# Weight splits and load-dependent work pinned in traced order, stores of split pairs two weights later, first loads reordered

## The chip, the cores and the metric

One core of a Trainium2 chip runs the kernel. Its engines are TensorE (PE in the profile; PEld are its weight loads), VectorE (DVE), ScalarE (ACT), GpSimd (POOL) and SyncE (SP, which here only issues DMAs). The metric is the device time of one execution in microseconds (us). Before the change it is 2699.4 us, the median of three runs from 2695.46 to 2699.83.

## The reference

One layer of a hybrid decoder, in float32, for a prompt of 2048 rows and a sample batch of 8 x 4 rows. The width D is 1024, the MLP's is 4096.

```python
xn = rms_norm(x, norm_mix_pre)
qk_raw, v_m, o_m, gates, q_a, k_a, v_a = split_projection(xn @ w_in)
y_m = mlstm_output(mlstm(short_conv(qk_raw), v_m, gates), o_m, mlstm_norm)
y_a = rms_norm(sliding_window_attention(q_a, k_a, v_a, attn_sinks), attn_norm)
x = x + rms_norm(concatenate([y_m, y_a]) @ w_out, norm_mix_post)
u = rms_norm(x, norm_ffn_pre)
f = square(relu(u @ w_up)) @ w_down
x = x + rms_norm(f, norm_ffn_post)
x = x + sigmoid(x @ w_pgate) * (p @ w_pproj)
```

The new recurrent states and attention caches are outputs too. (The calls in the third and fourth line are shortened.)

## The kernel before

**Products in three passes.** A float32 product is made of values split into a rounded part and a rest: `hi = round(v)`, `lo = v - hi`. TensorE then adds hi x hi, hi x lo and lo x hi (`mm3`). So every weight tile is split once (`wsplit`, L247): ACT casts it to hi (L248), DVE or POOL subtracts (L249). `weng` (L242) gives the subtraction to DVE and POOL in turn, unless the caller names one.

**The ring of weights.** `Ring` hands out the split pairs in the order of a plan that covers the whole program. There are PAIRS = 7 slots of pairs and RAWS = 5 of raw loads. `take(n)` (L323) makes as many weights ready as LOOK or LOOKR say beyond n; both are 0, so a weight's load and split are traced where it is used. A weight that is used again is stored as a pair in DRAM (`keep`, L266, the DMA `wk<-w` at L268 on POOL's queue) and loaded from there later (`w<-wk`, L274, SP). Tiles are named by their number in the ring: w305 is the pair, wr310 a raw load, wb3130 and wb3131 are the two wide raw tiles of an up step, 302 to 312 the weights of step 5 of the first group, and re050, hh0500, hl0510, dn0511 belong to that step.

**Stages.** The 16 blocks of 128 prompt rows are projected in six chunks (w_in, attention and mLSTM, up to about 700 us). Then come three groups of blocks, each with the output projection (`mix`), the MLP and the gated embedding (`gate`). The first group makes and stores its split weights, the two others load them. The MLP has 16 steps; each multiplies two column blocks of w_up and adds into f through two row blocks of w_down. From step FAST on (2, 4 and 2 in the three groups) the two chunks of a group share seven products instead of eight (`up_both`, L1670): sums of the weights' quarters are built by POOL and DVE (`Ring.product`, L284) and sums of the activations by `sums()` (L1620). The fourth product's weight (key 3) makes two pairs from one quarter: first a by-product, `self.last`, then a subtraction on POOL (L303), then the pair itself.

**What sets the order.** `Flow.issue` pins TensorE's instructions in traced order (`keep_in_program_order`). All other instructions are put in order by a scheduler below the kernel, engine by engine, and each engine and queue then runs its own strictly in that order. Side work (`mix_post`, `gate_post`, `gate_embed`, `sums`, attention, mLSTM) are generators; each `yield` says how many us of TensorE's work are traced before it goes on.

**Also touched.** `fetch` and `project` load and norm the prompt rows (the scaling of a block is at L584, its factor x0t on POOL at L499, the sum of squares on ACT at L497, SP's load at L456). `weights` in the mLSTM adds a mask to Wt (L927) behind a load. The sample's state work loads `sso` (L1255, POOL's queue) and takes a tanh (L1256, ACT). `finish` (L1792) stores the outputs, `gate_embed` (L1830) loads and transposes p.

## Time and profile before

| | |
|---|---|
| median of three runs | 2699.4 us |
| the profiled execution's own time | 2696.58 us |
| its span | 2694.8 us |
| mean granted TensorE clock | 0.979 |
| instructions | 39194 |
| DMA | 626.98 MB, mean 233 GB/s |

The profile shows one execution. A row of a timeline has the start, the length, the engine, the line and operation, out<-in without numbers, and in brackets the idle time before it with what ended it. A row of waits has an engine's line, what released it, the total, the number of times and the longest. The granted clock is a share of full speed; the kernel's 0.979 is a mean over stretches at full and at half speed. TensorE's busy time counts instructions that run at half clock as busy.

### The profile page before, as it was taken

The numbers are of one execution on the slowest core, as the hardware profiler recorded it, in microseconds if no ns is written. First come the engines' busy times: TensorE is split into PE (matmuls) and PEld (weight loads), VectorE is DVE, ScalarE is ACT, GpSimd is POOL, SyncE is SP. The second block draws the span as 40 slices with busy tenths as digits, with TensorE's granted clock in tenths as the row PEclk, the third lists the DMA queues.
The fourth block names the chain that finished last, engine by engine and source line by source line (L and its number), as shares of the span: only waits on it lengthen the run. The fifth ranks groups of instructions, "written<-read, shape, count | busy, mean of one in ns | idle before, by whom it ended". The sixth has DMA issues, their size and how long they took to land.

```text
span 2694.8 us, 39194 instructions
## 1 busy us (share of the span) xinstructions
PE 2550.8 (95%) x14284; PEld 2221.0 (82%) x14284; DVE 1475.1 (55%) x3112; ACT 982.1 (36%) x2163; POOL 635.4 (24%) x928
## 2 busy tenths in 40 slices
PE   4899999999899999999898998999999998999997
PEld 4788878788678888888787887889998878999985
DVE  3665756655667666666643446444446345444452
ACT  3554554544545444433422423222223133222241
POOL 3510111112434666665623130000001010000010
PEclk9899999999899999999999998999999999999999
DMA  7756566576786666665798731555556896777786
GB/s 235 272 204 209 196 195 212 187 263 238 260 316 210 254 248 252 247 248 220 273 354 274 253 93 56 172 188 193 188 188 223 299 328 220 256 256 257 259 293 218
DMA packets 219409, 626.98 MB, mean 233 GB/s; under 512 B 33141, under 2 KB 65097, under 8 KB 219200
## 3 DMA queue, kind: packets, MB, share of 16 engines
q1 hardware_dynamic: 173392, 465.77, 51.4%
q0 software_dynamic: 45776, 158.68, 15.2%
q8 instruction: 113, 1.85, 0.3%
q14 instruction: 80, 0.66, 0.1%
q10 hardware_dynamic: 48, 0.03, 0.0%
HBM read 470.22 MB, written 155.25 MB: 232 GB/s over the span
## 4 chain that ended last, share of the span: by engine, by line
PE 68%; DVE 9%; DMA 7%; issue 7%; POOL 5%; ACT 3%; SPq 0%; POOLq 0%; DVEq 0%; ACTq 0%
PE dn L145 18%; PE up L145 18%; PE mo L145 5%; PE pg L145 4%; PE v L145 3%; PE o L145 2%; POOL w L249 2%; PE qk L145 2%; PE gv L145 2%; PE qa L145 1%; PE aT L149 1%; PE aO L145 1%; DMA wk<-w 1%; DVE hl L228 1%; PE aS L145 1%
## 5 line engine op out<-in xcount | busy, mean ns | idle before, releaser
L145 PE MATMUL dn<-w,hh 128*128 128x512 f32 x1792 | 572.3, 401 | 22.6 <-DVE f L1718 16.9
L145 PEld LDWEIGHTS dn<-w,hh 128*128 128x128 f32 x1792 | 335.3, 191 | 105.6 <-DVE f L1718 23.1
L1718 DVE TENSOR_TENSOR f<-f,dn 128x512 f32<-128x512 f32 x420 | 285.8, 686 | 221.4 <-PE dn L145 220.9
L145 PE MATMUL dn<-w,hl 128*128 128x512 f32 x896 | 356.8, 398 | 4.3 <-DVE hl L228 4.1
L1682 DVE TENSOR_TENSOR re<-up,re 128x384 f32<-128x384 f32 (+1 forms) x280 | 144.0, 514 | 289.3 <-PE up L145 289.2
L145 PEld LDWEIGHTS dn<-w,hl 128*128 128x128 f32 x896 | 170.4, 190 | 45.4 <-DVE hl L228 5.9
L268 POOL DMA_DIRECT2D wk<-w x242 | 133.9, 555 | 108.4 <-DVE w L249 85.3
L1683 ACT COPY re<-up 128x384 f32<-128x384 f32 (+1 forms) x40 | 17.9, 448 | 379.6 <-PE up L145 379.6
L228 DVE TENSOR_TENSOR hl<-re,hh 128x384 fp32r<-128x384 f32 (+1 forms) x192 | 120.3, 627 | 62.3 <-ACT hh L227 61.6
L1608 ACT ACTIVATE re<-re 128x384 f32<-128x384 f32 (+1 forms) x160 | 78.8, 493 | 170.6 <-DVE re L1682 168.3
L248 ACT CAST w<-wb 128x512 fp32r<-128x512 f32 x98 | 60.6, 621 | 200.9 <-PE dn L145 128.4
L248 ACT CAST w<-wr 128x512 fp32r<-128x512 f32 (+1 forms) x152 | 93.6, 620 | 103.2 <-issue 22.3
L249 POOL TENSOR_TENSOR w<-wr,w 128x512 fp32r<-128x512 f32 (+1 forms) x76 | 103.1, 1357 | 95.0 <-ACT w L248 87.2
L1432 POOL TENSOR_TENSOR f<-f,gffn 128x512 f32<-128x512 f32 x16 | 21.0, 1321 | 430.2 <-ACT j L1430 429.8
L249 POOL TENSOR_TENSOR w<-wb,w 128x512 fp32r<-128x512 f32 x70 | 90.1, 1298 | 106.8 <-ACT w L248 106.4
L249 DVE TENSOR_TENSOR w<-wr,w 128x512 fp32r<-128x512 f32 (+1 forms) x76 | 80.3, 1058 | 43.6 <-ACT w L248 41.1
L1026 DVE CUSTOM_DVE_ANT_0 s<-aS,cst,sink 128x256 f32<-128x256 f32 (+1 forms) x128 | 56.9, 472 | 75.4 <-PE aS L145 75.2
L1609 ACT ACTIVATE re<-re 128x384 f32<-128x384 f32 (+1 forms) x192 | 94.9, 495 | 6.0
L227 ACT CAST hh<-re 128x384 fp32r<-128x384 f32 (+1 forms) x192 | 92.5, 482 | 6.8
L1032 ACT ACTIVATE s<-s,swt 128x257 f32<-128x257 f32 (+1 forms) x128 | 63.3, 496 | 72.3 <-DVE swt L1029 71.4
L145 PE MATMUL up<-ut11h,w 128*128 128x384 f32 x320 | 88.8, 340 | 0.0
L1615 POOL CAST hh<-hh 128x16 fp32r<-128x16 f32 x32 | 7.1, 222 | 338.2 <-ACT hh L227 338.1
(1525 smaller groups left out, 6538.6 us busy)
## 6 DMA issues: line engine op xcount, KB each, us to landing
w<-wk SPq DMA_DIRECT2D x678, 512.0 KB, 4.8
wk<-w POOLq DMA_DIRECT2D x238, 512.0 KB, 5.8
wr<-in_w_down_dram SPq DMA_DIRECT2D x64, 256.0 KB, 6.8
wb<-in_w_up_dram SPq DMA_DIRECT2D x28, 512.0 KB, 5.8
w<-wk SPq DMA_DIRECT2D x20, 528.0 KB, 4.1
x<-in_x_prompt_dram SPq DMA_DIRECT2D x16, 512.0 KB, 4.2
y<-yd SPq DMA_DIRECT2D x32, 256.0 KB, 5.8
xr<-in_x_prompt_dram SPq DMA_DIRECT2D x16, 512.0 KB, 9.2
```

The lines of the kernel that those rows point to most:

```text
L145: ins = self.pe.matmul(out, lhsT, rhs, start=start, stop=stop)
L227: act.copy(hi, src)
L228: dve.tensor_tensor(lo, src, hi.bitcast(F32), ALU.subtract)
L248: act.copy(hi, src)
L249: (eng or weng()).tensor_tensor(lo, src, hi.bitcast(F32), ALU.subtract)
L268: put(self.kept[key], t.bitcast(U32))
L1026: dve.tensor_tensor_reduce(s_[:, s, lo : 2 * P], pS[:, s, lo:], bias[:, j, lo:], 1.0 if s == 0 else 0.0625, sink[:, h : h + 1], ALU.add, A ...
L1032: act.activation(e_, e_, AF.Exp, bias=nm[:, s : s + 1], accum_out=sm[:, s : s + 1])
L1608: act.activation(t, src, AF.Relu)
L1609: act.square(t, t)
L1682: add = lambda out, a, b: dve.tensor_tensor(out, a, b, ALU.add)
L1718: dve.tensor_tensor(out(i), out(i), ps[i], ALU.add)
```

## The change

- `wsplit` pins both halves of a split, and `Ring.take` makes AHEAD = 2 weights beyond those asked for, everywhere. So a split stands where it is traced, two weights before its use.
- `Ring.keep` no longer stores at once: `store` issues a pair's DMA when STORE = 2 more tiles were taken, pinned too.
- The first chunk's x1 and x2 are loaded ahead of the first weights, and normed later.
- Pinned as well: the mask add of Wt, the copies of the attention caches to the output, the tanh of sso.
- In `sums()`, the seven adds of the second half (q = 1) go from DVE to POOL in the second and third group.
- `finish` stores the last chunk's outputs from SP's queue; `gate_embed` loads all tiles of p first, yields EMBW = 3.0 us, and then transposes.

Where instructions stand now, at three places. The first is DVE's queue at the start of the program (x0t is the norm factor of block 0, x00t its first transpose, w2 to w6 are weights of the gates and values and of the attention's queries). Before:

```order
L498 TENSOR_SCALAR x0t_181<-x0t_181 128x1
L249 TENSOR_TENSOR w2_195<-wr2_196,w2_195 128x528
L249 TENSOR_TENSOR w4_211<-wr4_212,w4_211 128x528
L498 TENSOR_SCALAR x1t_223<-x1t_223 128x1
L498 TENSOR_SCALAR x2t_231<-x2t_231 128x1
L249 TENSOR_TENSOR w6_386<-wr6_387,w6_386 128x512
L584 SCALAR_TENSOR_TENSOR x0_90<-x0_90,x0t_181,gpre_159 128x1024
L228 TENSOR_TENSOR x0l0_239<-x00t_241,x0h0_237 128x4x128
L228 TENSOR_TENSOR x0l1_240<-x01t_248,x0h1_238 128x4x128
L584 SCALAR_TENSOR_TENSOR x1_221<-x1_221,x1t_223,gpre_159 128x1024
```

Now:

```order
L507 TENSOR_SCALAR x0t_181<-x0t_181 128x1
L507 TENSOR_SCALAR x1t_243<-x1t_243 128x1
L507 TENSOR_SCALAR x2t_249<-x2t_249 128x1
L593 SCALAR_TENSOR_TENSOR x0_90<-x0_90,x0t_181,gpre_159 128x1024
L251 TENSOR_TENSOR w2_198<-wr2_199,w2_198 128x528
L593 SCALAR_TENSOR_TENSOR x1_187<-x1_187,x1t_243,gpre_159 128x1024
L593 SCALAR_TENSOR_TENSOR x2_189<-x2_189,x2t_249,gpre_159 128x1024
L251 TENSOR_TENSOR w4_213<-wr4_215,w4_213 128x528
L230 TENSOR_TENSOR x0l0_257<-x00t_259,x0h0_255 128x4x128
L230 TENSOR_TENSOR x0l1_258<-x01t_266,x0h1_256 128x4x128
L251 TENSOR_TENSOR w6_231<-wr6_233,w6_231 128x512
```

The scaling of x0, which TensorE's first transpose reads, stood behind the splits of w2, w4 and w6; it stands ahead of all of them now, behind the factors of x1 and x2.

The second is ACT's queue in step 5 of the first group's MLP, at the end of the down pass of step 4 and the first products of step 5 (up051 is the first product, w305 and its by-product w306 come from key 3). Before:

```order
L248 CAST w304_10115<-wb3020_10068 128x512
L1608 ACTIVATE re040_9768<-re040_9768 128x384
L1609 ACTIVATE re040_9768<-re040_9768 128x384
L227 CAST hh0410_9934<-re040_9768 128x384
L248 CAST w306_10137<-wb3021_10070 128x512
L248 CAST w305_10136<-wb3021_10070 128x512
L248 CAST w307_10181<-wb3020_10068 128x512
L248 CAST w308_10207<-wb3021_10070 128x512
L1683 COPY re050_10062<-up051_10066 128x384
L248 CAST w309_10232<-wr309_10233 128x512
```

Now:

```order
L250 CAST w304_10079<-wb3020_9966 128x512
L1696 COPY re050_10074<-up051_10078 128x384
L250 CAST w306_10102<-wb3021_9968 128x512
L250 CAST w305_10100<-wb3021_9968 128x512
L1620 ACTIVATE re051_10075<-re051_10075 128x384
L1621 ACTIVATE re051_10075<-re051_10075 128x384
L229 CAST hh0500_10124<-re051_10075 128x384
L250 CAST w307_10144<-wb3020_9966 128x512
L250 CAST w308_10163<-wb3021_9968 128x512
```

The casts of w305 to w308 stood ahead of re050, the evacuation of the first product; they stand behind it now.

The third is DVE's queue at the end of the same products and the start of the down pass (up053 is the last product; dn0500 is the first down product, its weights are w309 and w310). Before:

```order
L249 TENSOR_TENSOR w310_10239<-wr310_10240,w310_10239 128x512
L1682 TENSOR_TENSOR re050_10062<-up056_10114,re050_10062 128x384
L228 TENSOR_TENSOR hl0500_10111<-re051_10063,hh0500_10110 128x384
L1682 TENSOR_TENSOR re052_10064<-up057_10135,re050_10062 128x384
L249 TENSOR_TENSOR w312_10253<-wr312_10254,w312_10253 128x512
L1682 TENSOR_TENSOR re053_10065<-up054_10158,re052_10064 128x384
L249 TENSOR_TENSOR w313_10361<-wb3130_10362,w313_10361 128x512
```

and, three rows further on:

```order
L249 TENSOR_TENSOR w314_10384<-wb3131_10364,w314_10384 128x512
L1682 TENSOR_TENSOR re050_10062<-up053_10206,re050_10062 128x384
L228 TENSOR_TENSOR hl0511_10203<-re052_10064,hh0511_10202 128x384
L1718 TENSOR_TENSOR f0_7746<-f0_7746,dn0500_10260 128x512
L228 TENSOR_TENSOR hl0510_10229<-re050_10062,hh0510_10228 128x384
L1718 TENSOR_TENSOR f1_7747<-f1_7747,dn0501_10268 128x512
L1718 TENSOR_TENSOR f2_7748<-f2_7748,dn0502_10276 128x512
```

Now:

```order
L1695 TENSOR_TENSOR re050_10074<-up055_10189,re050_10074 128x384
L1695 TENSOR_TENSOR re050_10074<-up053_10217,re050_10074 128x384
L230 TENSOR_TENSOR hl0511_10214<-re052_10076,hh0511_10213 128x384
L251 TENSOR_TENSOR w310_10218<-wr310_10220,w310_10218 128x512
L230 TENSOR_TENSOR hl0510_10241<-re050_10074,hh0510_10240 128x384
L1731 TENSOR_TENSOR f0_7758<-f0_7758,dn0500_10272 128x512
L251 TENSOR_TENSOR w312_10251<-wr312_10253,w312_10251 128x512
L251 TENSOR_TENSOR w313_10258<-wb3130_10260,w313_10258 128x512
L251 TENSOR_TENSOR w314_10267<-wb3131_10262,w314_10267 128x512
L1731 TENSOR_TENSOR f1_7759<-f1_7759,dn0501_10280 128x512
L1731 TENSOR_TENSOR f2_7760<-f2_7760,dn0502_10288 128x512
```

w310's low half stood behind the second product's evacuation and stands behind the last one's now; those of w312, w313 and w314 stood among the products and stand between f0 and f1 now. On POOL, the first sum of the wide tiles of the step after next (wb3240, L298, traced two steps ahead) stood behind w311's low half and stands ahead of it now. On ACT, the tanh of sso stood between the evacuations f6 and f7 of the second group's output projection (L1521) and stands 82 rows further on, in the MLP.

```diff
--- before.py
+++ after.py
@@ -67,8 +67,9 @@
 MIXW = 6.0
 LODVE = 2
 STEPS = FF // (FS * P)
-LOOK = 0
-LOOKR = 0
+AHEAD = 2
+STORE = 2
+EMBW = 3.0
 RAWS, PAIRS = 5, 7
 
 
@@ -199,6 +200,7 @@
     pe = Flow(tc)
     swa, mls, tsp = pe.side(), pe.side(), pe.side()
     dma, put = nc.sync.dma_start, nc.gpsimd.dma_start
+    here = tc.keep_in_program_order
 
     xp = A["x_prompt"].rearrange("b t d -> (b t) d")
     xs = A["x_sample"].rearrange("b t d -> (b t) d")
@@ -245,8 +247,8 @@
         return dve if turns % LODVE == 0 else pool
 
     def wsplit(hi, lo, src, eng=None):
-        act.copy(hi, src)
-        (eng or weng()).tensor_tensor(lo, src, hi.bitcast(F32), ALU.subtract)
+        here(act.copy(hi, src))
+        here((eng or weng()).tensor_tensor(lo, src, hi.bitcast(F32), ALU.subtract))
 
     class Ring:
 
@@ -256,7 +258,7 @@
             self.raw = es.enter_context(tc.tile_pool(name=nm + "raw", bufs=raws))
             self.pair = es.enter_context(tc.tile_pool(name=nm + "pair", bufs=pairs))
             self.n = 0
-            self.plan, self.ready, self.kept, self.uses = None, [], {}, {}
+            self.plan, self.ready, self.kept, self.uses, self.later = None, [], {}, {}, []
 
         def tile(self, n):
             self.n += 1
@@ -265,11 +267,18 @@
 
         def keep(self, key, t):
             self.kept[key] = dram.tile(list(t.shape), U32, name=f"{self.nm}k{len(self.kept)}")
-            put(self.kept[key], t.bitcast(U32))
+            self.later.append((self.n, key, t))
+
+        def store(self):
+
+            while self.later and self.later[0][0] + STORE <= self.n:
+                _, key, t = self.later.pop(0)
+                here(put(self.kept[key], t.bitcast(U32)))
 
         def get(self, key, n, make):
 
             t = self.tile(n)
+            self.store()
             if key in self.kept:
                 dma(t.bitcast(U32), self.kept[key])
             else:
@@ -322,7 +331,7 @@
 
         def take(self, n=1):
 
-            while len(self.ready) < n + (LOOK if n > 2 else LOOKR):
+            while len(self.ready) < n + AHEAD:
                 key, make = next(self.plan, (None, None))
                 if make is None:
                     break
@@ -598,8 +607,9 @@
     def fetch(ci):
 
         for b in CHUNKS[ci]:
+            if b not in xq:
+                xq[b] = load_x(xp[b * P : (b + 1) * P, :], P, f"x{b}")
             if b > 0:
-                xq[b] = load_x(xp[b * P : (b + 1) * P, :], P, f"x{b}")
                 norm_x(xq[b], P, f"x{b}")
         if ci == len(CHUNKS) - 1:
             xq["s"] = load_x(xs, NS, "xs")
@@ -634,6 +644,8 @@
 
         if ci == 0:
             norm_x(xq[0], P, "x0")
+            for b in blocks[1:]:
+                xq[b] = load_x(xp[b * P : (b + 1) * P, :], P, f"x{b}")
         wg = by2(ring.take(4))
         Kh = pw.tile([P, 2, (CMAX + 1) * P], F32R, tag="Kh", name=f"Kh{ci}", bufs=2)
         Kl = pw.tile([P, 2, (CMAX + 1) * P], F32R, tag="Kl", name=f"Kl{ci}", bufs=2)
@@ -924,7 +936,7 @@
         def weights(i):
             Wt = sm.tile([P, MH, P], F32, tag="Wt", name=f"Wt{blocks[i]}")
             dma(Wt, bc(r["mbd"][:, i * P : (i + 1) * P], 0, P))
-            dve.tensor_tensor(Wt, Wt, bc(mask, 1, MH), ALU.add)
+            here(dve.tensor_tensor(Wt, Wt, bc(mask, 1, MH), ALU.add))
             for h in range(MH):
                 act.activation(Wt[:, h], Wt[:, h], AF.Exp, bias=cq(i, 0, h), scale=-1.0)
             Ws[i] = Wt
@@ -1110,7 +1122,7 @@
         for out, cache, off in ((12, "cache_swa_k", Z_KA), (13, "cache_swa_v", Z_VA)):
             oc = O[out].rearrange("l b s k d -> (l b) s (k d)")
             cc = A[cache].rearrange("l b s k d -> (l b) s (k d)")
-            put(oc[:, 0 : WIN - DT, :], cc[:, DT:WIN, :])
+            here(put(oc[:, 0 : WIN - DT, :], cc[:, DT:WIN, :]))
             put(oc[:, WIN - DT : WIN, :], zsd[:, off : off + 128].rearrange("(b t) c -> b t c", t=DT))
 
 
@@ -1253,7 +1265,7 @@
             yield 1.0
         so = sp.tile([NS, 512], F32, name="sso")
         put(so, zsd[:, Z_O : Z_O + 512])
-        act.activation(so, so, AF.Tanh, scale=0.5)
+        here(act.activation(so, so, AF.Tanh, scale=0.5))
         dve.tensor_scalar(so, so, 0.5, 0.5, ALU.mult, ALU.add)
         y = sp.tile([NS, 512], F32, name="sym")
         mlstm_finish(num, col[:, 8:12], so, y, NS, "dm")
@@ -1628,19 +1640,20 @@
                 c = slice(q * n, (q + 1) * n)
                 (b11, b21), (b12, b22) = [[[y[:, :, c].bitcast(F32) for y in b] for b in B[ci]] for ci in range(2)]
                 t1, t2, t4 = [temp(f"ts{i}{q}", n) for i in range(3)]
-                dve.tensor_tensor(t1, b12[0], b11[0], ALU.subtract)
+                eng = pool if q and gi > 0 else dve
+                eng.tensor_tensor(t1, b12[0], b11[0], ALU.subtract)
                 yield TSP
-                dve.tensor_tensor(t4, b12[1], b11[1], ALU.subtract)
+                eng.tensor_tensor(t4, b12[1], b11[1], ALU.subtract)
                 yield TSP
-                dve.tensor_tensor(t1, t1, t4, ALU.add)
+                eng.tensor_tensor(t1, t1, t4, ALU.add)
                 yield TSP
-                dve.tensor_tensor(t2, b22[0], t1, ALU.subtract)
+                eng.tensor_tensor(t2, b22[0], t1, ALU.subtract)
                 yield TSP
-                dve.tensor_tensor(t2, t2, b22[1], ALU.add)
+                eng.tensor_tensor(t2, t2, b22[1], ALU.add)
                 yield TSP
-                dve.tensor_tensor(t4, b21[0], t2, ALU.subtract)
+                eng.tensor_tensor(t4, b21[0], t2, ALU.subtract)
                 yield TSP
-                dve.tensor_tensor(t4, b21[1], t4, ALU.add)
+                eng.tensor_tensor(t4, b21[1], t4, ALU.add)
                 yield TSP
                 for i in (1, 0, 2):
                     h, l = [y[:, :, c] for y in T[i]]
@@ -1789,7 +1802,7 @@
         dve.tensor_tensor(rs, rs, rq[:n, i, 0:1], ALU.mult)
         residual(b, rs, x)
 
-    def finish(b, half, pg, pv, n, nm):
+    def finish(b, half, pg, pv, n, nm, last):
         hs = slice(half * 512, half * 512 + 512)
         t = gw.tile([P, 512], F32, tag="sg", name=f"sg{nm}{half}")
         act.activation(t[:n], pg, AF.Tanh, scale=0.5)
@@ -1797,7 +1810,7 @@
         o = gw.tile([P, 512], F32, tag="ot", name=f"ot{nm}{half}")
         dve.scalar_tensor_tensor(o[:n], t[:n], 0.5, f[b][:n, hs], ALU.mult, ALU.add)
         dst = y_s[:, hs] if b == "s" else y_p[b * P : (b + 1) * P, hs]
-        put(dst, o[:n])
+        (dma if last else put)(dst, o[:n])
 
     def gate_post(gi, ci, c, sample):
 
@@ -1834,16 +1847,18 @@
         pl = gw.tile([P, 2, CMAX * P], F32R, tag="pl", name=f"pl{gi}{ci}")
         xt["p", ci] = (ph, pl)
         sample = sample and ci == 1
-        for i, b in enumerate(c):
-            t = gw.tile([P, PD], F32, tag="p", name=f"p{b}")
+        ts = [gw.tile([P, PD], F32, tag="p", name=f"p{b}", bufs=CMAX + 1) for b in (*c, "s")[: len(c) + sample]]
+        for t, b in zip(ts, c):
             dma(t, pp_in[b * P : (b + 1) * P, :])
+        if sample:
+            dma(ts[-1][:NS], ps_in)
+        yield EMBW
+        for i, (t, b) in enumerate(zip(ts, c)):
             transpose_split(t, ph[:, :, cols(i)], pl[:, :, cols(i)], ps_m, f"pt{b}")
             yield 1.0
         if sample:
-            t = gw.tile([P, PD], F32, tag="p", name="ps")
-            dma(t[:NS], ps_in)
             xt["ps"] = gw.tile([P, 2, 2 * NS], F32R, tag="sp", name="sp_", bufs=1)
-            transpose_split_s(t, xt["ps"], 2, ps_m, "pts")
+            transpose_split_s(ts[-1], xt["ps"], 2, ps_m, "pts")
 
     def gate_mm(gi, ci, c, sample, ready):
 
@@ -1889,11 +1904,11 @@
                     for e in range(2):
                         mm2s(pgS, xt["s"][:, k + e], w[e], k + e == 0, k + e == KT - 1)
             for i, b in enumerate(c):
-                finish(b, half, pgs[i], pvs[i], P, f"{b}")
+                finish(b, half, pgs[i], pvs[i], P, f"{b}", sample)
             if sample:
                 jg = gw.tile([P, 512], F32, tag="jg", name=f"jg{half}", bufs=1)
                 join_s(jg[:NS], pgS, 512, f"jg{half}")
-                finish("s", half, jg[:NS], jv[:NS], NS, "s")
+                finish("s", half, jg[:NS], jv[:NS], NS, "s", True)
 
     for gi, chunks in enumerate(GROUPS):
         sample = gi == len(GROUPS) - 1
```

## The prediction

> **What bounds the kernel.** I read the page's busy times first, then the list of TensorE's waits, then the windows.
>
> ```profile
> PE 2550.8 (95%) x14284; PEld 2221.0 (82%) x14284; DVE 1475.1 (55%) x3112; ACT 982.1 (36%) x2163; POOL 635.4 (24%) x928
> ```
>
> PE is busy 2550.8 of 2694.8 us, so 144 us of the span are its waits and its tail. The change removes no matmul and shortens none; it can only move these waits or make new ones. Where they are (engine and line, what was waited for: us in total, times, longest):
>
> ```profile
> PE x00t L149 <- DVE x L584: 25.6, 1, 25.6
> PE dn L145 <- DVE f L1718: 16.9, 14, 8.1
> PE gv L145 <- ACT x0h L227: 8.8, 2, 8.6
> PE aT L149 <- DVE s L1036: 8.2, 5, 3.5
> PE mo L145 <- ACT f L1521: 6.8, 1, 6.8
> PE dn L145 <- ACT ju L1470: 4.5, 1, 4.5
> PE dn L145 <- DVE hl L228: 4.1, 2, 2.3
> PE pt5t L149 <- DMA p<-in_p_prompt_dram: 4.0, 1, 4.0
> PE mS L145 <- DVE m14f L906: 3.9, 1, 3.9
> PE qk L145 <- DVE w L249: 3.7, 1, 3.7
> ...
> PE pt2t L149 <- DMA p<-in_p_prompt_dram: 2.1, 1, 2.1
> ```
>
> Most are single events. A wait also costs clock behind it, which windows show (columns: stretch, length, busy times, then the granted clock):
>
> ```profile
> 73.00:105.00 32.00, 21.06 (x96) 19.68 (x96) 25.57 (x56) 12.44 (x31) 17.85 (x24) 0.79 0.83 292
> 951.43:1300.00 348.57, 340.94 (x1686) 303.92 (x1686) 215.24 (x291) 140.77 (x258) 216.27 (x237) 1.00 0.63 236
> 1300.00:1345.00 45.00, 37.26 (x164) 29.72 (x163) 36.14 (x64) 22.70 (x52) 25.10 (x28) 0.89 0.84 305
> 1440.00:1465.00 25.00, 16.38 (x56) 12.38 (x55) 1.02 (x2) 3.25 (x8) 9.37 (x13) 0.80 0.74 225
> 1665.00:1700.00 35.00, 26.91 (x115) 22.73 (x115) 23.98 (x32) 7.32 (x12) 0.00 (x0) 0.85 0.39 135
> 2065.00:2090.00 25.00, 21.38 (x109) 17.00 (x108) 21.16 (x40) 9.44 (x22) 6.81 (x7) 1.00 0.79 265
> ```
>
> So 32 us at 0.79 are 6.7 us lost beside the waits. The fast MLP steps of the first group (951 to 1300) are the opposite: PE idles 7.6 us in 349 and runs at full clock. That stretch has the least to win and, with fresh splits of 11 weights in each step of some 32 us, the most to lose.
>
> **The change, part by part.** All sums are against the profiled execution, 2696.58 us (span 2694.8), 2.8 below the median of the three runs, 2699.4.
>
> *The start.* On DVE, ACT and POOL:
>
> ```profile
> 23.40 0.92 DVE L249 TENSOR_TENSOR w<-wr,w 128x512 fp32r<-128x512 f32 x1 [5.50 <-ACT w L248]
> 24.24 1.27 DVE L584 SCALAR_TENSOR_TENSOR x<-x,x0t,gpre 128x1024 f32<-128x1024 f32 x1
> 6.44 0.61 POOL L499 TENSOR_TENSOR x0t<-x0t,nhalf 128x1 f32<-128x1 f32 x1
> 14.27 1.06 ACT L497 ACTIVATE x1j<-x 128x1024 bf16<-128x1024 f32 x1 [0.73 <-DMA x<-in_x_prompt_dram]
> 39.46 1.06 ACT L497 ACTIVATE x3j<-x 128x1024 bf16<-128x1024 f32 x1 [11.29 <-DMA x<-in_x_prompt_dram]
> ```
>
> x0's factor is ready at 7.05, but its scaling stands behind w6's split and starts at 24.24. Now it stands ahead of w2's, behind x1t and x2t, whose tiles are loaded ahead of the weights. I take 3 to 5 us for those two tiles behind x0, so PE's first transpose comes near 12.6 instead of 25.57: 13 us. The 8.6 us at gv came from x3j (L497) ahead of an evacuation in ACT's queue; the casts of w5 and w6, whose loads stay late, stand there now. Term: **-13**. The two waits together are 34 us; at best about 20 go (the first 13, most of the second), at worst 6, if w5 and w6 come later still.
>
> *The mask adds.* DVE waited for a load in front of w14's split:
>
> ```profile
> 73.56 0.69 DVE L927 TENSOR_TENSOR Wt<-Wt,cst 128x512 f32<-128x512 f32 x1 [3.05 <-DMA Wt<-mbd]
> ```
>
> Pinned, the add stands behind the splits of w14 to w18. The qk wait (3.7) and its half-clock time (some 1.5) go; the two aT waits stay: **-5** (-12 if they go too, +2 if w18's split now delays s).
>
> *The tanh of sso.* ACT's queue:
>
> ```profile
> 1458.88 0.63 ACT L1256 ACTIVATE sso<-sso 32x512 f32<-32x512 f32 x1 [10.20 <-DMA sso<-zsd]
> ```
>
> The next COPY stood behind it. It now stands some 80 instructions later, in the MLP: 6.8 us and about half of the 5 us that 0.80 of 25 us cost: **-9** (-12 to -5).
>
> *First group's gate.* pt5t and pt2t waited 4.0 and 2.1 us for loads of p that were issued one after the other; they now come first, EMBW earlier. With the clock (0.89 of 45 us is 5 us) 11 us are at stake; xt transposes, now side by side, will wait 1 to 2 us for their splits: **-8** (-12 to 0).
>
> *Places at 697 to 705 and 784 to 830*, where m14f (3.9) and hl (4.1) were late behind splits: these stand ahead of the splits now, but w227, w251 and w252 stand in front of other evacuations: **-7** (-16 to +5).
>
> *Seven adds of sums() in each of groups 1 and 2 to POOL.* DVE at the 8.1 us wait:
>
> ```profile
> 1677.23 0.95 DVE L1663 TENSOR_TENSOR tl<-tl,tl 128x768 f32<-128x768 f32 x1
> 1678.97 0.68 DVE L1718 TENSOR_TENSOR f<-f,dn 128x512 f32<-128x512 f32 x1
> ```
>
> DVE gives off 7 x 0.95 = 6.6 us. POOL takes 1.29 us for 512 elements (below), so an estimated 1.9 for 768, 13 us in a row, and the casts on ACT and the low halves on DVE wait for it; in the new order another evacuation goes behind them. In group 2 hh of the second chunk stands behind such casts, a new wait of 2 to 6 us; on the other side the 4.5 us behind ju (L1470) go, since hh2001 now stands ahead of it. Together **+3** (-14 to +18). *The other gates and the last six stores on SP*: **-4** (-6 to 0). All these make -43.
>
> *The fast steps, 14 of them.* This is where the pinned splits cost.
>
> ```profile
> 962.11 0.62 ACT L248 CAST w<-wb 128x512 fp32r<-128x512 f32 x1 [2.78 <-POOL wb L303]
> 965.67 0.48 ACT L1683 COPY re<-up 128x384 f32<-128x384 f32 x1 [1.46 <-PE up L145]
> 974.06 0.56 DVE L1682 TENSOR_TENSOR re<-up,re 128x384 f32<-128x384 f32 x1 [0.69 <-PE up L145]
> 976.14 0.56 DVE L1682 TENSOR_TENSOR re<-up,re 128x384 f32<-128x384 f32 x1 [0.73 <-PE up L145]
> 962.20 0.69 DVE L1718 TENSOR_TENSOR f<-f,dn 128x512 f32<-128x512 f32 x1 [0.71 <-PE dn L145]
> 968.40 2.03 DVE L249 TENSOR_TENSOR w<-wr,w 128x512 fp32r<-128x512 f32 x1
> 972.67 0.69 DVE L249 TENSOR_TENSOR w<-wr,w 128x512 fp32r<-128x512 f32 x1
> 980.40 0.54 DVE L228 TENSOR_TENSOR hl<-re,hh 128x384 fp32r<-128x384 f32 x1
> 959.41 1.29 POOL L249 TENSOR_TENSOR w<-wb,w 128x512 fp32r<-128x512 f32 x1 [7.89 <-ACT w L248]
> 960.78 1.29 POOL L303 TENSOR_TENSOR wb<-wb,wb 128x512 f32<-128x512 f32 x1
> 974.98 1.58 POOL L298 TENSOR_TENSOR wb<-wb,wb 128x512 f32<-128x512 f32 x1 [2.38 <-DMA wb<-in_w_up_dram]
> ```
>
> And PE's main wait in the whole stretch, 951 to 1300:
>
> ```profile
> PE dn L145 <- DVE f L1718: 7.2, 10, 0.8
> ```
>
> A product takes 976.14 - 974.06 = 2.08 us, six down matmuls 0.69 + 0.71 = 1.40 (0.23 each; an evacuation and the wait for the next). First, the fourth product's weight (w305 with its by-product w306): both casts stood ahead of COPY re050 on ACT, done while the down pass still ran (962.11). Now they stand behind it, so they begin when the first product ends. From there: COPY 0.48, cast 0.62, POOL low half 1.29, POOL subtraction 1.29, cast 0.62, low half 1.29, in all 5.6, with hand-overs 5.9. PE gets there after two products and two matmuls, 4.5: **1.4 us** waited. Second, w310's low half on DVE stood in the middle of the products (968.40); now it is behind the last product's evacuation and hl0511: 0.55 + 0.54 + 0.69 = 1.8 after PE has begun the down pass, which wants it after four matmuls, 0.9: **0.9 us**. Third, POOL's L298 add for the weights of the step after next now stands ahead of w311's low half. It waits for a load, which starts when w308 is split, now later; and DVE has the low halves of w312 to w314 between f0 and f1, each 0.7 us alone and 2.0 beside a POOL operation. That is 0 to 2.6 us at dn0510 and dn0511, in place of the old 0.7 at dn0511 (7.2 us over 10); I take 1.5, the middle, since the load's landing decides. Each step: 1.4 + 0.9 + 1.5 - 0.7 = 3.1; times 14 **+43** (bounds 14 x 1.6 = +22 and 14 x 4.2 = +59). The cover that is gone is the 16.6 us of down matmuls (72 x 0.23) that used to hide the split chain.
>
> Two rules bear on this. DVE's 2.03 us for an operation of 0.69 falls on a POOL operation of the same time. The Trainium skill (SBUF — State Buffer, "SBUF: two separate sides") says that both share one port pair as an exclusive lock, so that whoever comes second stands still; by it the adds moved to POOL spare DVE nothing while both are busy, and the +3 above would be about +7. The clock: the gate at 2065 to 2090, where PE idles 3.6 of 25 us, has 1.00; the stretch at 1440, with the 6.8 us wait, has 0.80. The same skill (TensorE: Matmul & The Clock Gate, "Part 1: The HAM clock gate") gives half rate after one idle window of about 3.4 us; by it waits of 1.4 us would cost no clock at all. The trace agrees here in part; the rival below has the other half.
>
> Sum: -43 + 43, so 2696.6; the runs of before lie up to 2.8 above their profiled one, and half of that gives **2698**.
>
> **Rivals.**
> - *Hidden losses, faster.* The loss per step stays at the firm 2.3 us less 0.7, or below, because the load lands early and f1 no longer waits: +22. With -43 that is 2675; with the start's best case 2668. For it: idle time of 144 us is there, and DVE (55%) and POOL (24%) have room. Against it: the order puts two POOL operations and two casts between the first and the fourth product in each step.
> - *Dear fast steps, slower.* One mechanism: POOL's L298 add waits for the load in front of w311's low half. It decides if the load lands later than 4.5 us into the down pass. Then each step loses 4.2, +59, and if the waits also bring half clock for 3.4 us (1.7 us lost) in half the steps, +12 more: 2696.6 - 43 + 59 + 12 = 2725. For it: half clock does follow several of the waits listed above (0.79, 0.80, 0.85, 0.89). Against it: those waits are 3 us and longer, and 2065 to 2090 keeps 1.00.
> - *The change moves nothing that counts.* The pins could leave the order as it was: the order says otherwise for a third of the splits. What could hold is that the start is bound by its loads, so that what is won at 25 us is waited out before 135. Then -43 shrinks to -32, and the time is 2709.
>
> **The numbers.** Chances: balance (2684 to 2712) 0.40, hidden losses (2660 to 2684) 0.32, dear steps (2712 to 2735) 0.20, loads (2700 to 2712) 0.08. A measurement of this kernel can tell about 0.2%, 5.4 us, from no change: under 2694 is faster, over 2704.8 slower. Of the balance a good third lies below, some 0.14, and a quarter above, 0.10. Faster 0.32 + 0.14 = 0.46; slower 0.20 + 0.10 + 0.05 = 0.35 (the loads' case reaches over the line with 0.05); the same 0.16 + 0.03 = 0.19. The range leaves a tenth at each end: 2662 to 2728; the likeliest case's own is 2684 to 2712.
>
> **What would show it.** Right: the first transpose near 12 to 13 us; no 6.8 us wait at mo; in each step of 951 to 1300 a wait of 1.2 to 1.6 us of up on POOL w and one near 0.9 of dn on DVE w; steps of 34 to 36 us instead of 32.3. Wrong: steps that stay near 32.3 (then the kernel is faster by some 40), a granted clock below 0.97 in those steps (then it is slower), or a first gv that still starts near 27.

## The result and the profile after

The changed kernel takes 2763.57 us, the median of four runs (2761.16 to 2768.24), against 2697.43 us for the kernel before (four runs, 2689.86 to 2699.83): a ratio of 1.0252 with a 95% interval of 1.0226 to 1.0279. The profiled execution took 2765.58 us, its span is 2763.8. It is 66 us slower than before, outside the range of the prediction.

The page of the changed kernel, engines and granted clock:

```profile
PE 2583.8 (93%) x14284; PEld 2223.2 (80%) x14284; DVE 1463.8 (53%) x3098; ACT 967.4 (35%) x2163; POOL 664.1 (24%) x936
...
PEclk9999999999999999999999999999999998999999
```

PE has the same 14284 matmuls at nearly the same mean clock (0.977 and 0.979) and is "busy" 33 us longer. In the fast steps below it is busy 17 us longer (428.4 against 411.2) at a granted clock of 1.00 in both. So part of a wait shows as longer matmuls, not as idle time, and the loss is larger than the list of waits. The list of PE's waits (line, releaser: us in total, times, longest) has new names at the top:

```profile
PE up L146 <- POOL w L251: 19.6, 17, 7.9
PE dn L146 <- POOL w L251: 16.0, 12, 2.1
PE x00t L150 <- DVE x L593: 12.5, 1, 12.5
PE dn L146 <- DVE f L1731: 9.4, 8, 3.1
PE dn L146 <- DVE w L251: 7.1, 15, 0.5
PE dn L146 <- ACT re L1620: 6.9, 1, 6.9
...
PE spv L146 <- DVE qk1se L560: 3.9, 1, 3.9
PE up L146 <- ACT w L250: 3.9, 14, 0.3
...
PE pg L146 <- POOL w L251: 3.2, 1, 3.2
```

Before, PE waited for one split of a weight in the first 100 us and hardly again; now it waits for `w` on three engines, all through the program. Of the large old waits the one for x00t is half as long, the one of 8.6 us at gv has become one of 3.3, and the one for f at mo (6.8) is gone.

Where the 69 us between the two profiled executions arise is read from the start of one instruction per stage in both traces (us):

| start of | before | after | difference |
|---|---|---|---|
| first transpose (x00t) | 25.57 | 12.49 | -13.1 |
| second chunk's transposes (x30t) | 148.46 | 128.85 | -19.6 |
| fifth chunk's transposes (x120t) | 495.49 | 475.85 | -19.6 |
| first MLP product (up0000) | 784.34 | 778.21 | -6.1 |
| first fast step, step 2 (up021) | 866.39 | 863.43 | -3.0 |
| step 15 (up0151) | 1286.58 | 1328.92 | +42.3 |
| second group's output projection (mo106) | 1439.65 | 1492.90 | +53.3 |
| second group's MLP (up1000) | 1504.73 | 1551.53 | +46.8 |
| its step 4 (up141) | 1693.61 | 1755.02 | +61.4 |
| third group's MLP (up2000) | 2223.21 | 2289.84 | +66.6 |
| its step 2 (up221) | 2287.23 | 2359.77 | +72.5 |
| end of the last matmul | 2683.00 | 2757.02 | +74.0 |
| the execution | 2696.58 | 2765.58 | +69.0 |

Each difference against the row above is what a stage gained or lost. The tail after the last matmul gains 5 us.

**The fast steps.** Thirteen of them, from step 2 to step 15: the window before, then after.

```profile
866.39:1286.58 420.19, 411.22 (x2029) 365.81 (x2028) 262.74 (x351) 170.80 (x313) 262.09 (x286) 1.00 0.64 242
```

```profile
863.43:1328.92 465.49, 428.38 (x2029) 363.23 (x2028) 232.62 (x351) 162.23 (x312) 265.93 (x285) 1.00 0.58 219
```

420.19 / 13 = 32.32 us a step before and 465.49 / 13 = 35.81 after, at a granted clock of 1.00 in both. PE's waits in these steps, before:

```profile
PE dn L145 <- DVE f L1718: 8.5, 12, 0.8
PE up L145 <- DVE re L1682: 0.5, 1, 0.5
```

and after:

```profile
PE dn L146 <- POOL w L251: 15.3, 11, 2.1
PE up L146 <- POOL w L251: 9.6, 13, 0.7
PE dn L146 <- DVE w L251: 6.3, 13, 0.5
PE up L146 <- ACT w L250: 3.6, 13, 0.3
PE dn L146 <- DVE f L1731: 2.2, 5, 0.9
```

Step 5 of the changed kernel on ACT and POOL, from its first product's evacuation (timeline rows):

```profile
972.93 0.48 ACT L1696 COPY re<-up 128x384 f32<-128x384 f32 x1 [11.31 <-PE up L146]
973.31 0.62 ACT L250 CAST w<-wb 128x512 fp32r<-128x512 f32 x1
976.70 0.62 ACT L250 CAST w<-wb 128x512 fp32r<-128x512 f32 x1 [2.77 <-POOL wb L312]
...
974.02 1.28 POOL L251 TENSOR_TENSOR w<-wb,w 128x512 fp32r<-128x512 f32 x1 [9.93 <-ACT w L250]
975.38 1.29 POOL L312 TENSOR_TENSOR wb<-wb,wb 128x512 f32<-128x512 f32 x1
977.40 1.28 POOL L251 TENSOR_TENSOR w<-wb,w 128x512 fp32r<-128x512 f32 x1 [0.73 <-ACT w L250]
...
991.33 1.51 POOL L307 TENSOR_TENSOR wb<-wb,wb 128x512 f32<-128x512 f32 x1 [3.14 <-DMA wb<-in_w_up_dram]
992.81 1.72 POOL L251 TENSOR_TENSOR w<-wr,w 128x512 fp32r<-128x512 f32 x1
```

The first six are the chain of the fourth product: evacuation, cast of w306, its low half, subtraction, cast of w305, its low half, done at 978.68, 5.75 us after 972.93. POOL had stood idle for 9.9 us before it and ACT for 11.3. The last two are the sum for the step after next, for whose load POOL stood 3.1 us, and w311's low half behind it.

### The profile page after: what moved, and what is told of

Same layout as the page of the kernel before. It is cut to its first block, busy times and chain, and to the rows that moved or that the text cites. A ratio compares the mean times of both kernels' runs of the same rounds, so it can differ in the third digit from the quotient of the medians.

```text
span 2763.8 us, 39133 instructions
## 1 busy us (share of the span) xinstructions
PE 2583.8 (93%) x14284; PEld 2223.2 (80%) x14284; DVE 1463.8 (53%) x3098; ACT 967.4 (35%) x2163; POOL 664.1 (24%) x936
## 3 DMA queue, kind: packets, MB, share of 16 engines
q0 software_dynamic: 45392, 157.50, 14.6%
## 5 line engine op out<-in xcount | busy, mean ns | idle before, releaser
L146 PE MATMUL dn<-w,hh 128*128 128x512 f32 x1792 | 582.2, 403 | 42.7 <-POOL w L251 16.0
L251 POOL TENSOR_TENSOR w<-wr,w 128x512 fp32r<-128x512 f32 (+1 forms) x76 | 111.1, 1462 | 202.8 <-ACT w L250 179.9
L230 DVE TENSOR_TENSOR hl<-re,hh 128x384 fp32r<-128x384 f32 (+1 forms) x192 | 105.6, 550 | 97.5 <-ACT hh L229 97.0
L250 ACT CAST w<-wr 128x512 fp32r<-128x512 f32 (+1 forms) x152 | 88.5, 617 | 34.7 <-PE dn L146 13.1
L146 PE MATMUL up<-ut10h,w 128*128 128x384 f32 x320 | 89.4, 352 | 7.9 <-POOL w L251 7.9
L146 PE MATMUL up<-ut01h,w 128*128 128x384 f32 x288 | 81.8, 348 | 14.5 <-POOL w L251 10.3
```

The source lines that it names most:

```text
L146: ins = self.pe.matmul(out, lhsT, rhs, start=start, stop=stop)
L230: dve.tensor_tensor(lo, src, hi.bitcast(F32), ALU.subtract)
L250: here(act.copy(hi, src))
L251: here((eng or weng()).tensor_tensor(lo, src, hi.bitcast(F32), ALU.subtract))
```

## Experiments

The times of single runs below stand beside the changed kernel's four runs (2761 to 2768). The length of a fast step is always the time from step 2's first product to step 15's, divided by 13.

**Is it the pins of the splits, or the rest?** Two lines of `wsplit`:

```diff
-        here(act.copy(hi, src))
-        here((eng or weng()).tensor_tensor(lo, src, hi.bitcast(F32), ALU.subtract))
+        act.copy(hi, src)
+        (eng or weng()).tensor_tensor(lo, src, hi.bitcast(F32), ALU.subtract)
```

> The changed kernel with the two pins in wsplit taken away and all else kept (AHEAD = 2, STORE = 2, the other pins, the start). On ACT the casts of w305 to w308 then stand ahead of re050 again, and on DVE w310 stands among the products, as before the change. Theory A, the pins of the splits cost: fast steps of the first group back from 35.8 to 32.3 to 32.6 us each (-45), the gate of the first group -8 to -16, the 7.9 us wait at the first product of the second group's step 2 gone; 2763.6 - 70 = 2690, between 2680 and 2705. Theory B, the distance of two weights, the later stores or the other parts cost: fast steps stay at 35 and more, time over 2740.

Measured: 2673.48 us (four runs, 2667.72 to 2676.13), a ratio of 0.9923 (0.9899 to 0.9947) to the kernel before. That is 90 us below the changed kernel, more than theory A asked for, and 0.8% faster than before. Its fast steps:

```profile
854.11:1269.75 415.64, 413.00 (x2030) 365.18 (x2028) 248.08 (x351) 170.23 (x313) 261.64 (x286) 1.00 0.64 244
```

31.97 us a step. In the traces, the stretch from step 15 to the second group's output projection takes 148.2 us (164.0 in the changed kernel, 153.1 before), and the wait of 7.9 us in the second group is gone (its step 2 takes 53.0 us, 65.2 in the changed kernel, 53.9 before). Theory B falls: with AHEAD = 2, STORE = 2 and all other parts kept, no loss is left in the steps. All three places of theory A came out.

**Does a pin cost, or its place?**

```diff
-AHEAD = 2
+AHEAD = 3
```

> The changed kernel with AHEAD = 3 instead of 2, splits still pinned. The fourth product's casts then stand ahead of re050 and w310's low half ahead of the last product's evacuation, and the sum for the step after next behind w311. Theory A', a pin costs only where its place is too late for its use: fast steps 32.3 to 33.5 us each, time 2763.6 - 40 = 2724, between 2705 and 2735. Theory A'', a pinned split costs wherever it stands, since it holds up its queue: fast steps 34.5 us or more, time 2745 or more.

Measured: 2692.71 us (ten runs, 2687.72 to 2704.72), a ratio of 1.0004 (0.9988 to 1.0019): as fast as before, 71 us below the changed kernel, and better than expected. Its fast steps:

```profile
859.91:1267.76 407.85, 407.85 (x2029) 366.87 (x2028) 210.25 (x351) 165.73 (x312) 257.47 (x286) 1.00 0.65 249
```

PE is busy in every microsecond of the 13 steps, 31.37 us each, 0.95 less than before the change. So in these steps a pinned split costs nothing where it stands early enough; one weight more or less decides over 4.4 us a step. The second group's step 2 is back at 54.3 us, too. The rest of the kernel is not free of a price: e3 stays 19 us above e1, and its stretch from step 15 to the second group's output projection takes 158.7 us against e1's 148.2. What makes that was not looked into; PE's longest wait there is one of 4.8 us for a load of a stored pair.

**Are the waits of a fast step separate?** Two kernels take the pin away in the first group's fast steps only, one from the fourth product's two splits, one from the down weights' splits (in this second one the flag stays on through the first group's gate, whose splits are unpinned with it).

```diff
+        keep_at = (lambda ins: ins) if ring.loose else here
+        keep_at(act.copy(hi, src))
+        keep_at((eng or weng()).tensor_tensor(lo, src, hi.bitcast(F32), ALU.subtract))
...
                 elif i == 3:
+                    self.loose = self.fast
```

> The changed kernel with only the splits of the fourth product (w305 and w306, and those of the other fast steps) unpinned in the first group's fast steps; its casts stand ahead of re050 again, the down weights and the sum for the step after next stay where the changed kernel has them. If the three waits of a fast step are separate, the first (1.0 to 1.1 us in the profile of the changed kernel) goes and the two of the down pass stay: steps of 34.7 instead of 35.8, time 2763.6 - 15 = 2749. Rival: the chain behind it (w307, w308, the load that follows, the sum, w311) only waits at its next link, and w311's wait grows: steps of 35.4 and more, 2757 or more.

Measured: 2746.14 us, and 34.20 us a step. The products' phase goes back from 16.26 to 14.70 us (means over 11 steps, from the first product to the first down product), the down phase stays. PE's waits in its 13 steps:

```profile
PE dn L146 <- POOL w L252: 15.3, 11, 2.1
PE dn L146 <- DVE w L252: 6.3, 13, 0.5
PE dn L146 <- DVE f L1734: 1.9, 5, 0.6
```

The down pass waits for the splits as in the changed kernel, to a tenth. The first wait is separate, and worth 1.6 us a step, more than the 1.0 us that the list of waits has for it.

```diff
                 dma(raw, src)
+                self.loose = self.fast
                 wsplit(h, l, raw)
+                self.loose = False
```

> The changed kernel with only the down weights' splits unpinned in the first group's fast steps: w310 and w312 stand among the products again, w311 ahead of the sum for the step after next; the fourth product stays pinned and late. If the waits are separate: the two of the down pass (0.5 and 2.1 us in the profile) go, the 1.0 us of the fourth product stays, steps of 33.2 to 33.6, time 2763.6 - 34 = 2730. Rival: these waits come from the DMA of the wide tile alone, and move to another reader of it: steps of 34.8 and more, 2750 or more.

Measured: 2746.47 us, but 35.59 us a step: in the steps the rival's side, for another reason than it gave. Most of the 17 us that were gained lie behind the steps (from step 15 to the output projection -11.9 against the changed kernel; there the gate is unpinned too). ACT's queue in step 5:

```profile
982.89 0.62 ACT L251 CAST w<-wr 128x512 fp32r<-128x512 f32 x1 [0.70 <-issue]
987.53 0.62 ACT L251 CAST w<-wr 128x512 fp32r<-128x512 f32 x1 [4.01 <-DMA wk<-w]
988.05 0.52 ACT L1623 ACTIVATE re<-re 128x384 f32<-128x384 f32 x1
```

The cast of w312, now early again, writes into the slot of w305, seven weights back; w305 was split late, since it is still pinned behind re050, and its store had to land first. The activations of the step's last products stood behind that cast for 4 us. PE's waits in the 13 steps:

```profile
PE dn L146 <- DVE f L1734: 15.3, 15, 1.6
PE up L146 <- POOL w L252: 9.6, 13, 0.7
PE dn L146 <- ACT hh L229: 7.9, 12, 0.8
```

Those for w310 and w311 went, and as much came for f and hh, behind the late cast.

> e11_rows with STORE = 0. In e11 ACT stood 4.0 us in front of the cast of w312, whose slot in the ring is that of w305, until w305's store had landed (52.4 us of such waits in 13 steps), and hh of the last products stood behind that cast. If the later stores are the price there, w305 is stored right behind its split, the wait shrinks to some 2 us and steps get 1 to 2 us shorter: 33.6 to 34.6, time 2720 to 2735. Rival: the store's own time from issue to landing decides, not its place, and the wait on ACT stays over 3 us, steps of 35.2 and more.

The edit is `STORE = 0` in that kernel. Measured: 2750.68 us, 35.23 us a step. ACT's waits for stores in the 13 steps, e11 first, then e12:

```profile
ACT w L251 <- DMA wk<-w: 52.4, 20, 4.1
```

```profile
ACT w L251 <- DMA wk<-w: 48.1, 37, 5.5
```

The expectation failed: the earlier stores took 4 us of 52 away, and there are 37 shorter waits in place of 20. The median store takes 6.6 us from issue to landing in e11 and 6.7 in e12. That this time, behind a split that is itself late, sets the wait is the likely reading, as the rival has it; it is not shown, since the single stores were not followed, and why they land as late as they do was not looked into.

**The place of the stores in the changed kernel:**

```diff
-STORE = 2
+STORE = 0
```

> The changed kernel with STORE = 0: a pair's store is issued as soon as the next tile is taken, still pinned. Theory E: POOL then waits in its queue for a low half on DVE before the low halves behind it, and fast steps get longer by 0.5 to 2 us each, 2770 to 2790. Rival: the later store gave nothing, steps of 35.8 us as in the changed kernel, 2760 to 2767.

Measured: 2765.68 us, 36.01 us a step against 35.81. The rival holds: the later store is worth nothing that can be told.

**The adds of `sums()`.**

```diff
-                eng = pool if q and gi > 0 else dve
+                eng = dve
```

> The changed kernel with the seven adds of sums() back on DVE in the second and third group. Theory C, the adds on POOL make the 6.9 us wait on ACT re at 1727 and the 5 us at 2323: between the second group's step 2 and step 4 PE gets 4 to 8 us faster, in the third group 5 to 8, together 2750 to 2756 where the changed kernel has 2763.6. Rival: both waits are of the pinned splits and of loads; within 3 us of the changed kernel.

Measured: 2752.08 us, 11 below the changed kernel's median; theory C. In the traces the stretch from the second group's MLP to its step 4 is 4.9 us shorter than in the changed kernel (198.6 for 203.5) and that from the third group's MLP to its step 2 8.9 us (61.0 for 69.9). The second figure is clear of the scatter: among the changed kernel and its variants the stretch takes 59.0 to 61.2 us in the four with the adds on DVE and 69.9 to 72.9 in the eight with the adds on POOL (64.0 before the change). The first is not, since variants that pin the splits at a distance of two and have the adds on POOL take 198.5 to 203.6; in step 3 alone the two sets part, 45.7 to 46.2 against 47.2 to 50.2 (46.8 before). The wait of 8.1 us for f, which the move was to end, is back in e4; the changed kernel has waits of 6.9 and 3.1 us in its place. What the adds do on POOL is seen in the changed kernel, second group (POOL, ACT and DVE rows):

```profile
1726.08 2.42 POOL L1652 TENSOR_TENSOR ts<-ts,ut11l 128x768 f32<-128x768 f32 x1
1730.65 2.39 POOL L1656 TENSOR_TENSOR ts<-ut10l,ts 128x768 f32<-128x768 f32 x1
1733.07 0.83 ACT L1661 CAST t2h<-ts 128x768 fp32r<-128x768 f32 x1 [3.72 <-POOL ts L1656]
1733.81 0.48 ACT L1620 ACTIVATE re<-up 128x384 f32<-128x384 f32 x1
1731.31 2.55 DVE L1662 TENSOR_TENSOR t1l<-ts,t1h 128x768 fp32r<-128x768 f32 x1
1736.15 0.95 DVE L1675 TENSOR_TENSOR tl<-ut11l,ut11l 128x768 f32<-128x768 f32 x1
```

An add takes 2.0 to 2.5 us on POOL; DVE's operations of the same size take 2.55 beside it and 0.95 alone. ACT's cast waits 3.7 us for the seventh add, and the evacuation of a finished product stands behind that cast: the 6.9 us wait of PE.

**The cache copies.**

```diff
-            here(put(oc[:, 0 : WIN - DT, :], cc[:, DT:WIN, :]))
+            put(oc[:, 0 : WIN - DT, :], cc[:, DT:WIN, :])
```

> The changed kernel with the two copies of the attention caches unpinned, so that they go back to the first microseconds on POOL's queue. Theory D, the pinned copies (603 and 653 us) slow the sample's stores and loads there: the 3.9 us wait at spv goes and the stretch 600 to 700 gets 4 to 7 us shorter; the start gets 1 to 6 us longer, since 1 MB more moves beside the first weights. Rival: the stretch stays as it is within 1 us. Time 2757 to 2768 in both.

Measured: 2767.97 us. In the traces the start loses 13.4 us (the second chunk begins at 142.29 instead of 128.85) and the stretch from the fifth chunk to step 2 takes 379.2 instead of 387.6 us, 8.4 less; the wait at spv is gone. (The changed kernel and the five others with pinned copies and with splits pinned at a distance of two take 387.6 to 394.2.) The start paid more than expected, and the copies are not all that moved. On ACT the sum of squares of x3 stands ahead of block 1's evacuations again, as before the change, and waits there for its load:

```profile
35.09 1.06 ACT L506 ACTIVATE x3j<-x 128x1024 bf16<-128x1024 f32 x1 [13.44 <-DMA x<-in_x_prompt_dram]
36.41 0.59 ACT L229 CAST x0h<-x10t 128x512 fp32r<-128x512 f32 x1
```

PE's wait at gv, 8.6 us before the change, is back with 8.1. So the pin of the copies goes with 13 us won at one end and 8 lost at the other, but some 8 of the 13 come by this place in ACT's queue. What the copies' own transfers cost was not separated, at either end.

**Putting it together.** e1 with the adds on DVE:

> e1_unpin with the seven adds of sums() back on DVE. If the costs of the two parts add up (e4 gave 11 to 14 us on the changed kernel), 2673.5 - 12 = 2661, between 2656 and 2666. Rival: the pinned splits made the wait behind the adds, and without them the adds cost little: 2670 to 2676. (e1's own profile has a 7.5 us wait on ACT re at 1637, which speaks for the first.)

Measured: 2660.43 us (2658.82 to 2666.47), a ratio of 0.9879 (0.9857 to 0.9901). The two costs add up.

```diff
-            while len(self.ready) < n + AHEAD:
+            while len(self.ready) < n + (3 if self.pin else AHEAD):
...
             fast = s >= FAST[gi]
+            ring.pin = fast and gi == 0
```

> e6 with the pins back in the fast steps of the first group alone, and there three weights ahead. e3's fast steps took 31.4 us each, e1's 32.0, so 14 steps give -8: about 2653 (2648 to 2658) if a pin in the right place is better than none. Rival: e3's shorter steps came from what was done ahead of them (other places of the loads): steps of 32.0 as in e6, no change against e6 within 3 us.

Measured: 2659.80 us (2656.97 to 2661.04), ratio 0.9874 (0.9851 to 0.9897). The steps are 31.40 us as in e3, 7.5 us less for 13 of them, but the stretch from step 15 to the second group's output projection takes 154.0 us for e6's 148.0, and the runs as a whole cannot be told from e6. (The profiled executions differ by 9 us, but e6's was the slowest of its four.) The steps' part is shown, a gain of the whole is not.

> e7 with the two cache copies moved from 600 to 650 us to the start of the third group. Theory D (the copies sit in POOL's queue and beside the loads of the last projection chunk): the stretch from the last chunk (x120t) to the first MLP product (up0000), 299 us in e1 against 289 before, gets 5 to 8 us shorter, and the third group 0 to 3 longer: 2648. Rival: that stretch is longer for another reason (the sample's evacuations on ACT): no change within 2 us there.

The edit moves the two `put` calls to the top of the loop over groups, under `if gi == 2`. Measured: 2658.14 us (2656.32 to 2670.59), ratio 0.9876 (0.9847 to 0.9906). The stretch from x120t to up0000 takes 291.7 us instead of e7's 293.4, within what it varies among kernels with the same instructions there (293.4 to 299.3 in e1, e6 and e7). Theory D is not confirmed by this run. These three kernels, at 1.2% below the kernel before, are the fastest of the study.

## Why the prediction was wrong

It forecast no change, as a balance of -43 and +43. The half on which it spent most of its working was right; the other half was not.

- **The fast steps** (+43 forecast for 14): 35.81 - 32.32 = 3.49 us each, +49. The three waits came in the order and at the places named. Over 11 steps the products' phase is 1.56 us longer (1.4 forecast), the group of dn0500 1.05 (0.9), that of dn0510 1.60, and the old 0.6 at dn0511 goes. e10 shows that the first is separate, e1 and e3 that the splits' three waits go without the pin, or with the pin and one weight more of distance.
- **The half-clock rival**: with waits of up to 2.1 us in nearly every step, twelve of the 13 steps have a granted clock of 1.00. Step 13 has 0.95 and takes 37.8 us, since its wait for w311 was followed by 3.4 us at half clock (a PE row, then the window behind it):

```profile
1280.76 0.79 PE L146 MATMUL dn<-w,hh 128*128 128x512 f32 x1 [2.07 <-POOL w L251]
1280.76:1284.20 3.44, 3.44 (x8) 2.76 (x9) 0.69 (x2) 0.07 (x1) 3.35 (x6) 0.51 0.60 194
```

  So what the rival put at half of the steps came once, and cost some 2 us. The Trainium skill's rule (TensorE: Matmul & The Clock Gate, "Part 1: The HAM clock gate"), half rate after an idle window of about 3.4 us, agrees with the twelve steps and not with step 13, where a wait of 2.07 us was enough; steps 5 and 9 kept 1.00 behind waits of 2.10 and 2.08.
- **Start and mask adds** (-18): -19.6. x0's scaling starts at 11.15 us, ahead of w2's split. DVE's rows:

```profile
11.15 1.28 DVE L593 SCALAR_TENSOR_TENSOR x<-x,x0t,gpre 128x1024 f32<-128x1024 f32 x1
12.35 1.82 DVE L251 TENSOR_TENSOR w<-wr,w 128x528 fp32r<-128x528 f32 x1
```

  The first transpose is 13.1 us earlier, as forecast, and the first qk 15.3 us (55.16 for 70.44). The other 4.3 us fit the number of the mask adds (-5) by luck, not by their working: the waits of these qk products for splits were to go and grew from 4.3 to 7.9 us, and the waits at aT were to stay and fell from 6.9 to 1.2. And e2 shows that 13 of the whole go with the pinned cache copies. The working read x3j's new place on ACT from the order, without seeing that it goes with that pin, and it did not price the copies at all: neither here nor where e2 is 8 us shorter, beyond the fifth chunk.
- **The tanh of sso** (-9): -6.5. Right.
- **The places at 697 to 705 and 784 to 830** (-7): +16.7 from the fifth chunk to step 2, beyond the upper bound of +5. This is a step that failed. Unpinning the splits (e1) takes 10.7 of the 16.7 away, unpinning the copies (e2) 8.4; the two overlap, and the stretch varies by some 6 us.
- **The gate of the first group** (-8): from step 15 on +10.9, less one slow step 3.5: +7.4, beyond the upper bound of 0. With the splits unpinned (e1) that stretch is 4.9 us shorter than before the change, so loading p early does gain some 5, and the pinned splits of w_pgate and w_pproj took more away (PE pg <- POOL w, 3.2 us, among them).
- **Second group, steps 2 and 3**: not in the sum at all, +14.6 (203.5 us for 188.9), of which the adds have 4.9 (e4); +9.7 are left. These steps are not fast, and unlike the others of the group they split fresh weights. POOL's queue there:

```profile
1638.43 4.15 POOL L1304 DMA_DIRECT2D out_dram<-snr  x8 [2.21 <-DVE snr L1301]
1642.57 0.57 POOL L1309 DMA_DIRECT2D bias_s<-in_const_b_dram  x1
...
1646.48 1.62 POOL L1322 DMA_DIRECT2D ssnk<-in_attn_sinks_dram  x3
...
1648.94 1.27 POOL L251 TENSOR_TENSOR w<-wr,w 128x512 fp32r<-128x512 f32 x1
```

  A low half, pinned behind 17 DMA issues of the sample's work, starts at 1648.94; the product that needs it waits 7.9 us, and the granted clock of step 2 is 0.86 (0.95 before). e1 has no such wait.
- **The adds on POOL** (+3, bounds -14 to +18): +11.5 by e4's time, +13 by e1 and e6. The mechanism was right and the size wrong: an add, estimated at 1.9 us, took 2.0 to 2.5, and DVE's 0.95 us became 2.55 beside it. The Trainium skill's exclusive lock of the port pair (SBUF — State Buffer, "SBUF: two separate sides"), which the prediction weighed at +7, agrees with these rows and was nearer.
- **Other gates and tail** (-4): the tail gave 5, the rest took 7.

What failed are therefore terms of the sum of -43: the places (-7), the first group's gate (-8), and the second group's steps 2 and 3, which have no term. Together they came to +34 where -15 was written, 49 of the 69 us. The sum took each edit's gain at the place it was made for and charged the pins of the splits in full to the fast steps only, though the same two lines pin every split of the program; elsewhere it had them as a doubt within its bounds. e1 shows what they cost there: 10.7, 15.8 and, in step 2, 12.2 us come back without them. The adds took another 9 us more than written. The rival that ended slower (2725) had the right sign by the wrong mechanism: dearer fast steps made only 6 us of the difference.

## What to carry to other kernels

Pinning an instruction in a queue is a claim about its place against everything else in that queue, so its price has to be read at every place where the line is traced, not at the one it was tuned for. Count the chain from the last thing the pinned instruction now stands behind to its reader: where that chain (5.75 us here) is longer than the work in between (4.5 us), at least the rest is lost in every step (1.56 us here), and in these steps one tile more of distance took it away altogether. Work moved to an idle engine is not free if others in order stand behind its result, or if the two engines slow each other (0.95 us became 2.55 here). And a run that unpins one instruction can move others with it, as e2 did on ACT: look at the queues before giving the difference to the one.

## What the runs showed of the hardware

The stores that free a slot can pace the queue that fills it: in e11 an early cast stood 4.0 us for a store to land, and moving the store ahead changed 52.4 us of such waits to 48.1 only. DMA issues on POOL take 0.52 to 0.57 us each as they stand in the queue (4.15 us for 8), so the run of 17, with some longer ones, is a delay of 10.5 us for whatever computes behind it. Waits of about the same length are followed by half clock or not: in the changed kernel the wait of 2.07 us up to 1280.76 by a granted clock of 0.51 over 3.4 us and that of 2.81 us up to 1698.82 by 0.50 over 4 us, but those of 2.10 us up to 994.58 and of 2.38 us up to 794.36 by 1.00 over 4 us. And PE, in e3's steps, was busy for 407.85 of 407.85 us with waits for no one, while DVE, ACT and POOL were busy 210, 166 and 257 us: with these engines at 41 to 63% load, PE need not wait for them if the order is right.
